# The gate modulation of the second layer is asked for when attention begins

## The chip, the core and the metric

The kernel runs on one core of one Trainium2 chip. The metric is the device time of one execution in microseconds (us). TensorE (PE in the profile) does matrix products and transposes, VectorE (DVE) and ScalarE (ACT) elementwise work and reductions, GpSimd (POOL) some elementwise work, and SyncE (SP) issues nearly all DMA transfers. Each engine works through its own list of instructions in order, and so does each list of transfers.

## The reference

Two layers run one after the other on `x` (1024 rows of 1024). Each is one mixer with three groups of heads between two norms:

```python
def hybrid_layer(x, c_act, ...):
    mod = c_act @ w_mod + b_mod
    shift, scale, gate = jnp.split(mod[:, None, :], 3, axis=-1)
    h = rms_norm(x, pre_gain) * (1.0 + scale) + shift
    proj = h @ w_in                     # 3088 columns, cut into the three groups' inputs
    a_out = sliding_window_attention(aq, ak, av, sinks) * silu(ag)
    r_out = rms_norm(retention(rq, rk, rv)) * silu(rg)
    g_out = rms_norm(gated_linear_attention(gq, gk, gv, log_a), gn) * silu(gg)
    y = concat([a_out, r_out, g_out]) @ w_out
    return x + gate * rms_norm(y, post_gain)
```

`c_act` is one row of 1024, the same for both layers. `w_mod` has 3072 columns per layer: a third each for shift, scale and gate. Shift and scale are needed when a layer starts; the gate, multiplied with `post_gain`, is needed only when the layer's rows are written.

## The kernel before

**Order of a layer.** The 1024 rows are eight tiles of 128, handled as four pairs. For a layer, `layer(l)` writes in this order: the projections `gg` and `rg` with their SiLU gates; then retention (projections `rq`, `rk`, `rv`, one chunk for each tile); gated linear attention, GLA (`gqk`, `gv`, with `kv` in between); attention (`aq0`, `aq1` with the rotation in `attn_rot`, then `ag0`, `ag1` with the gate); and the output product with `w_out`. In the second layer the last output (`last_output`) uses fewer products, over sums and differences of blocks of `w_out` and of pairs of rows, which VectorE, ScalarE and GpSimd prepare (`sw_second`, `Pair`).

**Precision.** The large products are three passes over operands that were split into a rounded high part and the rest. Each weight unit of 256 columns is loaded in four transfers of 256 KB into staging buffers `st` (eleven of them, shared by all weights, those of the modulation too), then split: ScalarE or VectorE writes the high part (line 147 or 149) and VectorE or GpSimd the rest (line 535).

**The planner.** TensorE's order is the order in which the program is written out; the other engines' lists are put in order by a scheduler that simulates when work can run. The writing is itself planned. `clk` is a clock in planned microseconds that each matmul advances by its estimated cost. Work beside the large products lives in generators, the jobs. A job yields a lag, and `pump`, called after every seven 256-column matmuls, every four 512-column ones, or after a product, lets each job go on whose lag has passed on `clk`. Flags order jobs among themselves. The lags are the dictionary `L`: a key with `@1` is used where the layer is 1 (the second one), the plain key otherwise.

**The modulation.** `mod_third(l, j)` computes one third (j = 2 is the gate) in two halves of 512 columns. Each half has eight steps: a transfer of 256 KB of `w_mod` into `st`, and a multiply-add on VectorE into the accumulator `acc` (line 365; line 363 for a first step without bias), then lag `mod2`. After lag `mod3` TensorE adds `acc` over the partitions. For the gate GpSimd first clears `acc` (line 357), SP loads the bias row into it (line 358), and the result is multiplied with the post gain into `modg` (line 379); then lag `mod5`. `acc` has one buffer, so a half begins only when TensorE has read the half before. `mod_all(l, js)` is a job that runs thirds one after another, if wanted after a flag. In each layer it is started after the gates, that is, when retention begins; in the first layer a second job waits for the first's flag and computes shift and scale of the second layer.

```python
            for k in range(KT):
                wt = stage()
                dma("lwm", wt, wv[:, k, c0:c0 + 512])
                ...
                    V.scalar_tensor_tensor(acc, wt, c_act[:, k:k + 1], acc, ALU.mult, ALU.add)
                yield lat("mod2", l)
            yield lat("mod3", l)
```

**Other names that the prediction uses.** `attn_rot` multiplies projected queries with tables read from memory (line 861), shifts 32-row blocks by transfers on SP (line 877), and a later job splits them (lines 835 and 836); TensorE's scores need that split. `attn_q` does the softmax of one tile; its probabilities go to TensorE through ScalarE (line 147) and an affine select on GpSimd (line 937). Attention output is stored in memory, read back and gated (line 1584; lags `aq5` and `ag1`). Head norms of retention and GLA wait lag `hn1` before TensorE transposes them. `kept` (line 1335) copies a product that later sums need.

Of the kernel before, what the change touches and what calls it, by code (L numbers as in the profile page):

```python
# [20 lines left out]
DEPTH = 2  # L21
# [70 lines left out]
def trunk(ctx: ExitStack, tc: tile.TileContext, ins, cst, out):  # L92
# [200 lines left out]
    def mod_first(rws, between):  # L293
# [20 lines left out]
        for hh in range(2):  # L314
# [9 lines left out]
            for k in range(KT):  # L324
# [271 lines left out]
    def sw_second():  # L596
        drain()
        for k in range(4):
# [7 lines left out]
            sw_split("T4", k, s4, "t4")  # L606
            yield L["sw1"]
        for name in ("T2", "T3", "T4"):
# [48 lines left out]
    def pre(l, t, xt, early=False, soon=False):  # L657
# [186 lines left out]
    def attn_kv(l, t, pk):  # L844
        kr = t1()[:, 0:P]
        v = kv["v"]
        v[t] = gp.tile([P, P], F32, tag="va", name=nm("va"), bufs=VDB)
        A.activation(v[t], pk[:, 128:256], AF.Copy)
# [33 lines left out]
    def attn_run(l):  # L882

        for hf in range(2):
            for g in range(2):
                for t in range(4 * hf, 4 * hf + 4):
                    yield (lat("aq7" if hf else "aq1", l), ("q", l, hf, g))
                    yield (0.0, ("kT", l, t))
                    job(attn_q(l, t, g, kv[(hf, g)]))
# [570 lines left out]
    def layer(l):  # L1460
# [25 lines left out]
                load(l, "rq")  # L1486
            gates_done[l] += n

        job(mod_all(l, (2,)))
        if l + 1 < DEPTH:  # L1490
            job(mod_all(l + 1, (1, 0), ("mod", l, 2)))
        for p in range(NP_):
            job(gla_decays(l, p))
        G.memset(stR, 0.0)
# [71 lines left out]
            do_kv(p)  # L1566
        load(l, "ag0")
        job(attn_run(l))
        mx = {}

        def rows(d, hf, *i):
# [96 lines left out]

B2, B1, BS, BST, MMB, SMB = 10, 8, 11, 5, 3, 3
EN = {"shw0": "V", "shw1": "A", "shw2": "A", "shw3": "A", "slw0": "V", "slw1": "G", "slw2": "V", "slw3": "G", "sht2": "A", "sht3": "A", "sht4": "A", "slt2": "V", "slt3": "G", "slt4": "G", "sd": "V", "mh0": "A", "mh1": "A", "mh2": "A", "mh3": "A", "mf": "A", "ms0": "V", "ms1": "V", "ms2": "V", "ms3": "V", "yg0": "V", "yg1": "V", "ml0": "V", "ml1": "V", "ml2": "V", "ml3": "V", "mod0": "A", "mod1": "V", "qst": "S", "smh": "S", "sml": "S", "sm0": "S", "sm1": "S", "lao": "S", "sao": "S", "lmix": "S", "ssg": "S", "lsg": "S", "ssr": "S", "lsr": "S", "lx": "S", "sx": "A", "lw": "S", "lwm": "S", "whi0": "V", "whi1": "A", "whi2": "A", "whi3": "A", "wlo0": "V", "wlo1": "V", "wlo2": "V", "wlo3": "G", "xn0": "V", "xn1": "V", "hlo0": "V", "hlo1": "V", "rot0": "V", "rot1": "V", "rdec": "V", "kslo": "V", "qslo": "V", "vlo": "G", "kT": "A", "qT": "A", "sprev": "A", "pn": "G", "pf0": "A", "aoc": "A", "hng": "V", "mh": "A", "gso": "V", "mg": "V", "mgl": "V", "rT": "A", "rv": "A", "gv": "A", "gk": "A", "ak0": "V", "ak1": "V", "ak2": "V", "ak3": "V", "kd0": "G", "kd1": "G", "kd2": "G", "kx1": "G", "kx2": "G", "kx3": "V", "kx4": "V", "qb": "G", "stx": "V"}  # L1670
L = {"sw1": 0.4, "ld1": 1.2, "ld2": 1.2, "ld1@1": 1.2, "ld2@1": 1.27, "swW00": 0.0, "swT1": 0.0, "swW11": 0.4, "swW10": 0.5, "tt1": 8.0, "tt2": 1.75, "tb1": 24.5, "tb2": 0.75, "pf3": 13.2, "pf1": 6.35, "pf2": 4.16, "mod1": 4.6, "mod2": 4.0, "mod3": 13.29, "mod4": 7.04, "mod5": 3.36, "mod6": 9.04, "pre1": 7.44, "kv1": 3.1, "kv2": 2.11, "aq1": 6.0, "aq7": 6.0, "ag1": 5.44, "aq2": 2.4, "aq6": 5.2, "aq3": 10.21, "aq4": 7.36, "aq5": 3.6, "hn1": 8.93, "hn2": 2.85, "gz1": 11.18, "gz2": 8.13, "gl1": 2.76, "gd3": 15.9, "gc1": 0.62, "gc2": 1.94, "gc3": 1.33, "gc4": 0.87, "gc6": 0.86, "gc5": 1.14, "rc1": 0.8, "rc2": 1.09, "rc3": 5.87, "rc4": 2.51, "fin1": 7.28, "lay1": 1.13, "gc4@1": 0.93, "mod2@1": 4.0, "mod3@1": 15.1, "mod5@1": 3.36, "mod6@1": 4.11, "pre1@1": 7.44, "kv1@1": 2.79, "kv2@1": 5.28, "aq1@1": 4.8, "aq7@1": 5.28, "ag1@1": 6.25, "aq2@1": 0.82, "aq6@1": 6.0, "aq3@1": 10.9, "aq4@1": 4.4, "aq5@1": 5.15, "hn1@1": 8.12, "hn2@1": 2.85, "gz1@1": 15.91, "gz2@1": 10.94, "gl1@1": 4.6, "gd3@1": 15.9, "gc1@1": 0.48, "gc2@1": 1.94, "gc3@1": 1.33, "gc6@1": 0.86, "gc5@1": 1.04, "rc1@1": 0.37, "rc2@1": 0.84, "rc3@1": 1.9, "rc4@1": 2.79, "fin1@1": 4.28, "lay1@1": 1.7}
CHUNK = 7
LAG = 2
VDB = 8
FIN = 1

_INS = ["x", "c", "positions", "w_mod", "b_mod", "pre_norm_gain", "post_norm_gain", "w_in", "attn_sinks",
# [29 lines left out]
```

## Time and profile before

| | |
|---|---|
| time, median of 3 runs | 1003.25 us (1001.63 to 1004.74) |
| profiled execution, time | 1010.63 us |
| profiled execution, span | 1008.9 us |
| mean granted TensorE clock | 0.986 |
| attention of the second layer, last product on TensorE ends | 920.8 us into the span |

A row of the profile names an engine, a source line, an operation and the tiles (output<-inputs, without buffer numbers). `x8` counts merged instructions; a bracket gives the idle time before the first of them and what ended it. Tables of waits give the total, the number and the longest. A line is often that of a helper: 163 is every matmul, 178 every transpose, 147 every copy on ScalarE, 152 every transfer through `dma`. The time of one row starts at the span's start. Busy time of TensorE is modelled, since matmuls are pipelined.

### The profile page before, as it was taken

What the parts mean: (1) busy time and instruction counts of PE and PEld (TensorE: products, weight loads), DVE (VectorE), ACT (ScalarE), POOL (GpSimd) and SP (SyncE); (2) the same over time, 40 slices, a digit from 0 to 9 for tenths busy, and PEclk for the clock granted to TensorE, in tenths of its full rate; (3) what the DMA queues carried; (4) which work ended last, traced back from release to release, by engine and by line L of the source; (5) the groups of instructions that cost most, each with busy time, mean ns of one, the idle gap of its engine ahead of it and who ended that gap; (6) DMA issues with size and microseconds to landing.
All of it is one profiled execution on the core that took longest, in us unless ns stands there. A gap on an engine that the chain in (4) does not pass through costs nothing.

```text
span 1008.9 us, 19610 instructions
## 1 busy us (share of the span) xinstructions
PE 975.4 (97%) x7137; PEld 829.5 (82%) x7137; DVE 684.5 (68%) x1680; ACT 408.8 (41%) x1152; POOL 234.4 (23%) x275
## 2 busy tenths in 40 slices
PE   5899999899999999999999999999999999999897
PEld 1499999888998777778889999998899877777785
DVE  3789857757666778564578275785666577566876
ACT  2476311223322656632465232123332256663321
POOL 2310001223320234330112000113332034544100
PEclk8899999999999999999999999999999999999999
DMA  9942513623326355577655251353132434378883
GB/s 293 308 137 76 173 45 100 170 81 96 96 74 199 89 149 163 171 239 244 214 157 173 64 158 32 108 150 100 41 104 85 125 90 130 112 236 249 265 263 140
DMA packets 129836, 148.73 MB, mean 147 GB/s; under 512 B 14046, under 2 KB 94152, under 8 KB 129740
## 3 DMA queue, kind: packets, MB, share of 16 engines
q1 hardware_dynamic: 124044, 137.92, 45.3%
q10 hardware_dynamic: 5696, 9.56, 2.6%
q8 instruction: 56, 0.92, 0.4%
q14 instruction: 40, 0.33, 0.1%
HBM read 109.17 MB, written 36.18 MB: 144 GB/s over the span
## 4 chain that ended last, share of the span: by engine, by line
PE 80%; DVE 8%; DMA 7%; issue 2%; POOL 1%; ACT 1%; SPq 0%; POOLq 0%; DVEq 0%; ACTq 0%
PE mm L163 61%; PE aux L163 14%; PE aux L178 5%; DMA st<-in_w_in_dram 2%; DMA st<-in_w_out_dram 1%; POOL sm L638 1%; DMA xk<-in_x_dram 1%; DMA wm<-in_w_mod_dram 1%; DMA t<-aoS 1%; DVE arena L535 1%; DMA st<-in_w_mod_dram 1%; DMA t<-sgS 1%; DVE t L328 0%; DVE st L572 0%; DMA mixF<-t 0%
## 5 line engine op out<-in xcount | busy, mean ns | idle before, releaser
L163 PE MATMUL mm<-arena 128*128 128x256 f32 (+2 forms) x1824 | 299.2, 318 | 1.8 <-ACT arena L707 1.8
L163 PE MATMUL mm<-arena,arena 128*128 128x256 f32 (+2 forms) x1824 | 300.7, 318 | 0.0
L163 PEld LDWEIGHTS mm<-arena 128*128 128x128 f32 x1824 | 254.6, 191 | 26.5 <-issue 4.1
L163 PEld LDWEIGHTS mm<-arena,arena 128*128 128x128 f32 x1824 | 254.1, 189 | 25.5 <-issue 4.6
L638 POOL TENSOR_TENSOR sm<-sm,mhalf 128x1 f32<-128x1 f32 (+1 forms) x64 | 56.1, 877 | 347.0 <-DVE sm L637 328.6
L163 PE MATMUL mm<-arena,mx 128*128 128x512 f32 (+1 forms) x564 | 132.4, 392 | 2.9 <-ACT kept L1335 2.9
L163 PEld LDWEIGHTS mm<-arena,mx 128*128 128x128 f32 x564 | 103.1, 191 | 27.1 <-ACT kept L1335 3.3
L147 ACT ACTIVATE t<-aux 128x256 f32<-128x256 f32 (+2 forms) x124 | 55.7, 467 | 76.1 <-PE aux L178 64.8
L147 ACT ACTIVATE arena<-st 128x512 fp32r<-128x512 f32 x94 | 56.1, 626 | 59.1 <-DMA st<-in_w_in_dram 21.4
L535 POOL TENSOR_TENSOR arena<-st,arena 128x512 fp32r<-128x512 f32 x31 | 43.2, 1395 | 138.9 <-ACT arena L147 100.9
L926 POOL TENSOR_TENSOR smx<-smx,sm 128x512 f32<-128x512 f32 x32 | 36.1, 1127 | 124.3 <-DVE sm L925 116.1
L535 DVE TENSOR_TENSOR arena<-st,arena 128x512 fp32r<-128x512 f32 x77 | 59.5, 795 | 6.1 <-ACT arena L147 4.1
L922 ACT ACTIVATE smx<-smx,sm 128x129 f32<-128x129 f32 x128 | 49.9, 392 | 28.4 <-DVE sm L919 28.4
L178 PE MATMUL aux<-c_ident,t 128*128 128x128 f32 (+1 forms) x292 | 48.8, 285 | 7.6 <-DVE t L669 7.2
L365 DVE SCALAR_TENSOR_TENSOR acc<-st,c_act,acc 128x512 f32<-128x512 f32 x60 | 45.5, 759 | 12.6 <-DMA st<-in_w_mod_dram 12.1
L178 PEld LDWEIGHTS aux<-c_ident,t 128*128 128x128 f32 (+1 forms) x292 | 35.4, 145 | 15.2 <-DVE t L669 9.0
L701 ACT ACTIVATE t<-aux,mod,mod 128x128 f32<-128x128 f32 x68 | 25.9, 458 | 43.8 <-DVE t L1242 18.2
L970 ACT ACTIVATE t<-aux 128x256 f32<-128x256 f32 x32 | 12.3, 383 | 75.5 <-PE aux L163 63.4
L163 PEld LDWEIGHTS aux<-t,mx 32*128 32x128 f32 (+1 forms) x896 | 39.5, 187 | 3.8 <-issue 2.1
L163 PE MATMUL aux<-t,mx 32*128 32x32 f32 (+1 forms) x896 | 40.7, 273 | 0.0
L917 DVE COPY_PREDICATED smx<-c_curmask,aux 128x256 f32<-128x256 int32 x64 | 25.5, 447 | 18.8 <-ACT smx L147 15.3
L1242 DVE SCALAR_TENSOR_TENSOR t<-t,sm,t 128x512 f32<-128x512 f32 x32 | 24.0, 779 | 18.6 <-DMA t<-in_x_dram 11.9
(220 smaller groups left out, 1384.3 us busy)
## 6 DMA issues: line engine op xcount, KB each, us to landing
st<-in_w_in_dram SPq DMA_DIRECT2D x96, 256.0 KB, 3.1
st<-in_w_mod_dram SPq DMA_DIRECT2D x64, 256.0 KB, 3.3
st<-in_w_out_dram SPq DMA_DIRECT2D x52, 256.0 KB, 3.8
mx<-mixS SPq DMA_DIRECT2D x20, 512.0 KB, 6.2
mixS<-t SPq DMA_DIRECT2D x72, 128.0 KB, 2.3
wm<-in_w_mod_dram SPq DMA_DIRECT2D x12, 512.0 KB, 8.0
t<-in_x_dram SPq DMA_DIRECT2D x24, 256.0 KB, 4.8
t<-tabS SPq DMA_DIRECT2D x16, 256.0 KB, 3.7
```

Of the source, the lines that this page charges most:

```text
L147: A.activation(dst, src, AF.Copy)
L163: T.matmul(dst, lhsT, rhs, start=start, stop=stop)
L178: T.transpose(dst, src, idn)
L365: V.scalar_tensor_tensor(acc, wt, c_act[:, k:k + 1], acc, ALU.mult, ALU.add)
L535: e.tensor_tensor(lo, st, f(hi), ALU.subtract)
L638: G.tensor_tensor(r, r, mhalf[:, :w], ALU.pow)
L701: A.activation(hf[:, ks], at[kt], AF.Identity, scale=gain, bias=shift)
L917: V.copy_predicated(sv, curmask.unsqueeze(1).to_broadcast((P, 2, P)), pv[:, :, n // P - 1, :])
L922: A.activation(sm[:, h, :], sm[:, h, :], AF.Exp, bias=mx[:, h:h + 1], accum_out=sums[:, h:h + 1])
L926: eng("pn").tensor_tensor(sm[:, :, 0:128], sm[:, :, 0:128], rs.unsqueeze(2).to_broadcast((P, 4, P)), ALU.mult)
L970: A.activation(sq, po, AF.Square)
L1242: V.scalar_tensor_tensor(xt[j], yg[j], r, xt[j], ALU.mult, ALU.add)
```

## The change

A tuple `EARLY` names the layers in which the modulation jobs start where they did, after the gates. In the other layers they start after attention's job. With `EARLY = (0,)` the first layer keeps its place for both jobs, and the second layer's gate third moves behind `attn_run`. Twenty lags get other values; all but `sw1` and `swW11` are those of the second layer. `mod2@1` is also used by the shift and scale of the second layer, which are computed during the first. No instruction is added or taken away.

```diff
@@ layer(l), after the gates
-        job(mod_all(l, (2,)))
-        if l + 1 < DEPTH:
-            job(mod_all(l + 1, (1, 0), ("mod", l, 2)))
+        if l in EARLY:
+            job(mod_all(l, (2,)))
+            if l + 1 < DEPTH:
+                job(mod_all(l + 1, (1, 0), ("mod", l, 2)))
@@ layer(l), before the attention projections
         load(l, "ag0")
         job(attn_run(l))
+        if l not in EARLY:
+            job(mod_all(l, (2,)))
+            if l + 1 < DEPTH:
+                job(mod_all(l + 1, (1, 0), ("mod", l, 2)))
@@ the lags L, those that differ
-sw1 0.4    swW11 0.4   ld1@1 1.2   ld2@1 1.27  gc4@1 0.93  mod2@1 4.0  mod6@1 4.11  kv1@1 2.79  kv2@1 5.28  ag1@1 6.25
+sw1 0.06   swW11 0.63  ld1@1 1.32  ld2@1 1.34  gc4@1 0.74  mod2@1 1.44 mod6@1 6.28  kv1@1 3.84  kv2@1 5.81  ag1@1 7.51
-aq2@1 0.82 aq5@1 5.15  hn1@1 8.12  gz2@1 10.94 gd3@1 15.9  gc2@1 1.94  gc3@1 1.33   gc6@1 0.86  rc4@1 2.79  fin1@1 4.28
+aq2@1 1.8  aq5@1 6.14  hn1@1 17.56 gz2@1 9.15  gd3@1 9.54  gc2@1 1.83  gc3@1 1.17   gc6@1 1.72  rc4@1 4.83  fin1@1 5.35
+EARLY = (0,)
```

More of the change, by code (lines that the diff above doesn't have):

```diff
@@ new lines @@
+L = {"sw1": 0.06, "ld1": 1.2, "ld2": 1.2, "ld1@1": 1.32, "ld2@1": 1.34, "swW00": 0.0, "swT1": 0.0, "swW11": 0.63, "swW10": 0.5, "tt1": 8.0, "tt2": 1.75, "tb1": 24.5, "tb2": 0.75, "pf3": 13.2, "pf1": 6.35, "pf2": 4.16, "mod1": 4.6, "mod2": 4.0, "mod3": 13.29, "mod4": 7.04, "mod5": 3.36, "mod6": 9.04, "pre1": 7.44, "kv1": 3.1, "kv2": 2.11, "aq1": 6.0, "aq7": 6.0, "ag1": 5.44, "aq2": 2.4, "aq6": 5.2, "aq3": 10.21, "aq4": 7.36, "aq5": 3.6, "hn1": 8.93, "hn2": 2.85, "gz1": 11.18, "gz2": 8.13, "gl1": 2.76, "gd3": 15.9, "gc1": 0.62, "gc2": 1.94, "gc3": 1.33, "gc4": 0.87, "gc6": 0.86, "gc5": 1.14, "rc1": 0.8, "rc2": 1.09, "rc3": 5.87, "rc4": 2.51, "fin1": 7.28, "lay1": 1.13, "gc4@1": 0.74, "mod2@1": 1.44, "mod3@1": 15.1, "mod5@1": 3.36, "mod6@1": 6.28, "pre1@1": 7.44, "kv1@1": 3.84, "kv2@1": 5.81, "aq1@1": 4.8, "aq7@1": 5.28, "ag1@1": 7.51, "aq2@1": 1.8, "aq6@1": 6.0, "aq3@1": 10.9, "aq4@1": 4.4, "aq5@1": 6.14, "hn1@1": 17.56, "hn2@1": 2.85, "gz1@1": 15.91, "gz2@1": 9.15, "gl1@1": 4.6, "gd3@1": 9.54, "gc1@1": 0.48, "gc2@1": 1.83, "gc3@1": 1.17, "gc6@1": 1.72, "gc5@1": 1.04, "rc1@1": 0.37, "rc2@1": 0.84, "rc3@1": 1.9, "rc4@1": 4.83, "fin1@1": 5.35, "lay1@1": 1.7}
```

1 line of the change is left out of this document (removed).

## The prediction

> **What bounds the kernel now.** I read the page first, then who waits for TensorE and when, then busy time by stretch, and last the instructions around each wait. The busy rows name the bound:
>
> ```profile
> span 1008.9 us, 19610 instructions
> PE 975.4 (97%) x7137; PEld 829.5 (82%) x7137; DVE 684.5 (68%) x1680; ACT 408.8 (41%) x1152; POOL 234.4 (23%) x275
> ```
>
> TensorE issues in the order that the planner wrote and is busy 97%, so a change that moves work between other engines can only give back, or create, moments in which TensorE waits. These are all of its named waits in the second layer (from 500 us), and then those of the first layer's second half (215 to 540 us):
>
> ```profile
> PE mm L163 <- ACT kept L1335: 2.9, 1, 2.9
> PE aux L163 <- ACT t L147: 1.3, 1, 1.3
> PE aux L163 <- DVE stR L1194: 1.0, 1, 1.0
> PE aux L163 <- DVE t L1173: 0.4, 1, 0.4
> ...
> PE aux L178 <- DVE mx L1115: 0.3, 1, 0.3
> PE aux L163 <- DVE sm L637: 0.3, 1, 0.3
> ```
>
> So the second layer loses TensorE time in two places: 2.7 us where retention ends and 2.9 us where the last output begins. By stretch (columns: us, then busy time and count for PE, PEld, DVE, ACT, POOL, then granted clock, DMA share, GB/s):
>
> ```profile
> 600.00:700.00 100.00, 97.32 (x778) 91.35 (x778) 64.40 (x186) 26.64 (x58) 17.26 (x18) 1.00 0.34 102
> 800.00:900.00 100.00, 100.00 (x608) 72.75 (x607) 69.06 (x136) 63.04 (x207) 41.81 (x44) 1.00 0.46 135
> 670.00:690.00 20.00, 17.32 (x118) 14.86 (x118) 11.78 (x28) 6.64 (x15) 4.59 (x4) 1.00 0.62 179
> 850.00:950.00 100.00, 97.11 (x524) 71.74 (x523) 68.45 (x127) 52.84 (x155) 41.22 (x42) 0.98 0.68 203
> 940.00:950.00 10.00, 7.11 (x24) 5.38 (x23) 9.35 (x19) 4.35 (x9) 0.49 (x2) 0.83 0.69 212
> ```
>
> The first two rows are the stage that the work leaves (retention) and the one that it enters (attention). Attention has no TensorE wait, but ACT and POOL are over twice as busy there. The wait at retention's end, on TensorE, ScalarE and the SP queue:
>
> ```profile
> 680.77 0.72 PE L163 MATMUL aux<-t 64*128 64x128 f32 x8 [1.28 <-ACT t L147]
> ...
> 679.60 0.63 ACT L147 ACTIVATE arena<-st 128x512 fp32r<-128x512 f32 x1 [3.77 <-DMA st<-in_w_in_dram]
> 680.14 0.58 ACT L147 ACTIVATE t<-aux 128x512 f32<-128x512 f32 x1
> ...
> 655.57 0.33 SPq L152 DMA_DIRECT2D t<-srS  x1
> 662.68 0.33 SPq L152 DMA_DIRECT2D st<-in_w_mod_dram  x1
> 664.80 0.38 SPq L152 DMA_DIRECT2D st<-in_w_in_dram  x1
> ...
> SPq L358 <- POOL acc L357: 9.3, 1, 9.3
> SPq L152 <- DVE stR L1194: 7.0, 1, 7.0
> ```
>
> Read upward. TensorE waits for ScalarE's copy at 680.14 (queries and keys of a retention chunk). That copy stands behind a weight conversion that sat 3.77 us for its transfer. The weights come through the SP queue, which is in order, and that queue stood still twice for the modulation: 9.3 us for the bias row into the accumulator (line 358), and 7.0 us before the modulation weights at 662.68, with the next w_in load (664.80) behind them.
>
> **The change part by part.** *The moved job.* Sixteen weight loads of 256 KB, two bias rows, two gain rows, two POOL memsets, sixteen sums on VectorE (line 365), four TensorE matmuls and two products (line 379) leave the stretch from about 577 to 703 us and enter the one from about 787 us. On SP the twenty transfers are 20 x 0.33 = 6.6 us of issue time (the row at 662.68 has one), which attention's shifts and stores now queue among. The count of work is the same, so only waits count. Removed: the two SP blocks and the sums between the retention chunks. I take the whole idle time of the 670 to 690 row, 20.00 - 17.32 = 2.68, as gone: **-2.7**. Bounds: 0 (the conversions alone keep it) and -2.7 (there is no more).
>
> *Late sums in attention.* One accumulator buffer serves all halves, so a half's sums can start only after the half before it was multiplied on TensorE, and TensorE stands still if they aren't ready at its own place. Before, the planner put 3.36 + 8 x 4.0 + 15.1 = 50.46 of its microseconds between two halves; now 3.36 + 8 x 1.44 + 15.1 = 29.98. What a planned microsecond is on the chip:
>
> ```profile
> 300.22 0.95 PE L163 MATMUL aux<-c_ones,acc 128*128 128x1 f32 x8
> 361.40 0.95 PE L163 MATMUL aux<-c_ones,acc 128*128 128x1 f32 x8
> 429.42 1.05 PE L163 MATMUL aux<-c_ones,acc 128*128 128x1 f32 x8
> 488.70 0.95 PE L163 MATMUL aux<-c_ones,acc 128*128 128x1 f32 x8
> 639.14 1.02 PE L163 MATMUL aux<-acc,c_ones 128*128 128x512 f32 x2
> 701.83 1.02 PE L163 MATMUL aux<-acc,c_ones 128*128 128x512 f32 x2
> ...
> 674.62 0.74 DVE L365 SCALAR_TENSOR_TENSOR acc<-st,c_act,acc 128x512 f32<-128x512 f32 x1
> 397.13 0.74 DVE L365 SCALAR_TENSOR_TENSOR acc<-st,c_act,acc 128x512 f32<-128x512 f32 x1
> 398.39 1.19 DVE L365 SCALAR_TENSOR_TENSOR acc<-st,c_act,acc 128x512 f32<-128x512 f32 x1
> ```
>
> Gaps of 61.18 (300.22 to 361.40), 59.28 and 62.69 us for 50.46 planned give 1.17 to 1.24, so the new gap is an estimated 35.2 to 37.3 us. The slowest sums took 675.36 - 639.14 = 36.2 us in the second layer and 399.58 - 361.40 = 38.2 us in the first layer's attention. So the wait is between 0 and 38.2 - 35.2 = +3.0; I take **0**, since the second layer's own 36.2 lies in the middle of the new gap. The first half's accumulator is free long before, so its sums can be done ahead. The same shorter lag holds for the second layer's shift and scale (mod2@1 serves them too, in the first layer's time): again 0 to +3.0, taken as 0, covered by 0.6 us of waits in all in that part and by the fact that they are now asked for when the queue is emptier than in the row at 398.39.
>
> *The first scores.* The new loads stand in the SP queue before the four shifts of the first rotated queries, and its margin is small:
>
> ```profile
> 801.77 1.28 DVE L836 TENSOR_TENSOR mx<-t,mx 128x512 fp32r<-128x512 f32 x2
> 803.26 0.74 PEld L163 LDWEIGHTS aux<-kT,mx 64*128 64x128 f32 x12 [0.36 <-issue]
> ```
>
> The split ends at 803.05, the scores start at 803.26: 0.2 us. Two sums ahead of it on VectorE would cost 2 x 0.74 = 1.5 us. But aq2@1 goes from 0.82 to 1.8, which puts these scores 0.98 planned us later (1.1 to 1.2 by the same ratio). Between 0 and +1.5; taken as 0, since the lag pays for most of it.
>
> *The last output.* TensorE's longest wait, with the row before it, and the VectorE row that the delay runs through:
>
> ```profile
> 939.77 3.68 PE L163 MATMUL mm<-arena,ma 128*128 128x512 f32 x15
> 946.33 3.92 PE L163 MATMUL mm<-arena,mx 128*128 128x512 f32 x9 [2.89 <-ACT kept L1335]
> ...
> 909.26 0.69 DVE L1584 SCALAR_TENSOR_TENSOR t<-t,t 128x512 f32<-128x512 f32 x1 [2.27 <-DMA t<-aoS]
> ```
>
> After the wait the clock is 0.83 in that 10 us row: nine matmuls took 3.92, where nine of the fifteen before took 9/15 x 3.68 = 2.21, so the stop costs 2.89 + 1.71 = 4.6 us. VectorE is 9.35 of 10 busy there. It had stood 2.27 us at 909.26 for a read of stored attention output, with the splits of w_out behind it. ag1@1 (6.25 to 7.51) and aq5@1 (5.15 to 6.14) put that read and that product 2.25 planned us later, so the splits can pass them. Bounds: 0 and -4.6. I take half of the 2.27, **-1.1**: nearer to nothing, because VectorE's waits for w_out transfers in the same stretch remain.
>
> *The other lags* (head norm hn1@1 8.12 to 17.56, decays gd3@1 15.9 to 9.54, the gc, gz, kv, rc, ld and fin1 entries, sw1) add no instruction: they change at which pump a job's next part is written. A pump comes every four or seven matmuls, so steps under about a planned microsecond often change nothing; swW11 and mod6@1 have no reader that is waited for in the second layer. Taken as 0: the list of waits above has none between 703 and 940 us, and the cover is that slack. If longer-held head norms run the tile buffers short, retention's and GLA's ScalarE copies would be late next.
>
> **The sum.** -2.7 + 0 + 0 + 0 - 1.1 = -3.8 us. On the profiled execution (1010.63 us, 7.4 above the median of 1003.25) that is 1006.8; on the median, 1003.25 - 3.8 = 999.45, **999.5 us**. 0.3%, some 3.0 us, is about what a measurement of this kernel tells from no change.
>
> **The rivals.** *The wait stays* (no change). The conversion at 679.60 waits for w_in, not for modulation weights, and 670 to 690 us is also where three weight units arrive at once (DMA share 0.62). For: the first layer waits in the same place, and there too for a ScalarE copy behind a conversion:
>
> ```profile
> 199.62 1.23 PE L163 MATMUL aux<-t 64*128 64x128 f32 x8 [3.09 <-ACT t L147]
> 198.19 0.63 ACT L147 ACTIVATE arena<-st 128x512 fp32r<-128x512 f32 x1 [2.87 <-DMA st<-in_w_in_dram]
> ```
>
> Against: modulation runs beside that retention too. Time: 1003.25 - 1.1 = 1002.2.
>
> *The last output pays* (slower). If the second half's loads stand behind the shifts and stores of attention until about 890 us, its eight sums (8 x 0.74 = 5.9 us) fall on VectorE where it is the bound (9.35 of 10 busy), and each is then TensorE time: 1003.25 - 2.7 + 5.9 = 1006.5 (rounded up from 1006.45). For: DMA share is 0.68 from 850 to 950 us. Against: by the gap above the half ends near 787 + 2 x 37 = 861 us. It decides from the point where more than 2.7 us of sums, four of them, come after 890; with a blocked SP queue w_out would be late as well.
>
> *Two engines on one port.* VectorE's sum at 398.39 took 1.19 us against 0.74 while POOL was in a subtraction of 1.74, and an affine select in attention is as tight as this:
>
> ```profile
> 397.30 1.74 POOL L535 TENSOR_TENSOR arena<-st,arena 128x512 fp32r<-128x512 f32 x1 [0.44 <-ACT arena L147]
> 887.25 1.30 POOL L937 TENSOR_SCALAR_AFFINE_SELECT t<-t 128x512 f32<-128x512 f32 x1 [3.92 <-ACT t L147]
> 888.83 0.60 PE L163 MATMUL aux<-t,vd 128*64 128x256 f32 x4
> ```
>
> It ended at 888.55, 0.28 us before its matmul. Sixteen sums at POOL's 0.42 share meet it 6.7 times, at 0.45 us each 3.0 us: if all reach TensorE, 999.45 + 3.0 = 1002.5; in retention POOL's share is 0.17. This is the rule of the Trainium skill (SBUF — State Buffer, section "SBUF: two separate sides"): VectorE with two SBUF inputs and GpSimd take one port pair in turn, each for a whole instruction. By that rule the move is to the wrong stage; the trace agrees in the 1.19 us row, but TensorE had no wait there.
>
> **How the numbers follow.** Forecast 0.46 (995.9 to 1001.5), the wait stays 0.13, port 0.08, the last output pays 0.33, this last at 1004 to 1008. Faster takes the forecast and a little of the other two: 0.48; same, what they leave with the forecast's edge: 0.17; slower 0.35 (the last rival, and both late-sum waits together). Low end: -2.7 - 4.6 is 995.95, less the 1.6 by which the fastest run shown lies under the median: 994.3. High end: 1006.5 and the first scores' +1.5: 1008.0.
>
> **What the new profile would show.** Right: no named wait of TensorE between 660 and 703 us, no SP wait on the memset of line 357 there, sums (line 365) from about 775 to 860, no wait before the accumulator's matmuls, and a wait under 2.9 us where the last output begins. Wrong: a wait on line 147 still at retention's end; TensorE waiting for a line 365; scores waiting for line 836; or a stop before the last output longer than 2.9 us, with sums or w_mod loads after 880 us.

## The result, and the profile after

The changed kernel is slower: 1015.75 us median (4 executions, 1013.88 to 1018.53) against 1002.89 us (1001.63 to 1004.74) for the kernel before on the same chip, a ratio of 1.0129 with a 95% interval of 1.0099 to 1.0159. The prediction was 999.5 (994.3 to 1008.0). The profiled execution took 1016.71 us.

The execution of the kernel before that the prediction read (1010.63 us) turned out to be untypical: a later one of the same code (e1 below) took 1002.69 us. From here on "before" in comparisons of traces is that later one. Its span, and the longest of its waits of TensorE between 660 and 705 us, and then from 790 us to the end:

```profile
span 1001.0 us, 19610 instructions
...
PE aux L163 <- ACT t L147: 1.5, 1, 1.5
PE aux L163 <- DVE stR L1194: 0.4, 1, 0.4
...
PE mm L163 <- DMA a<-mixS: 1.5, 2, 1.0
```

The wait at retention's end is in both executions. The 2.9 us for `kept` ahead of the last output, on which I had put 1.1 us of gain and the low end of the range, is not: it is 0.3 us here, and two waits for a transfer stand near it.

The changed kernel's page begins with these rows (busy us and share by engine):

```profile
span 1015.0 us, 19619 instructions
...
PE 980.8 (97%) x7137; PEld 833.8 (82%) x7137; DVE 679.1 (67%) x1680; ACT 407.4 (40%) x1152; POOL 230.8 (23%) x275
```

The work and the shares are those of before. The longest of TensorE's waits, from 690 us on and then from 215 to 540 us (engine, tile and line, what it waited for; total, number, longest):

```profile
PE mm L163 <- ACT kept L1335: 2.6, 1, 2.6
PE aux L163 <- POOL t L937: 1.6, 2, 0.9
PE aux L163 <- DVE t L963: 0.4, 1, 0.4
PE aux L163 <- ACT t L1099: 0.4, 1, 0.4
...
PE aux L178 <- DVE mx L1115: 1.1, 1, 1.1
PE aux L163 <- DVE mx L1115: 0.9, 1, 0.9
PE aux L163 <- DVE stG L1137: 0.6, 1, 0.6
```

The old wait for line 147 at retention's end is gone. In its place stand small waits in both layers' GLA, two in attention behind GpSimd's affine select, and one at the last output. By stretch (busy time and count for PE, PEld, DVE, ACT, POOL, then granted clock, DMA share, GB/s):

```profile
600.00:700.00 100.00, 100.00 (x806) 94.87 (x805) 58.73 (x180) 26.41 (x56) 16.95 (x17) 1.00 0.21 63
670.00:690.00 20.00, 20.00 (x143) 17.90 (x141) 12.42 (x34) 7.47 (x17) 3.96 (x4) 1.00 0.54 163
800.00:900.00 100.00, 98.21 (x585) 70.55 (x586) 69.22 (x143) 59.48 (x193) 38.06 (x41) 1.00 0.50 154
945.00:957.00 12.00, 9.36 (x29) 7.07 (x29) 10.68 (x22) 4.16 (x9) 0.60 (x2) 0.73 0.68 209
```

Where the time came from, stage by stage. The table gives how much later than before the same event is on the chip, worked out from the starts of the same rows in the two traces.

| event | before, us | changed: later by |
|---|---|---|
| first layer, last masked retention scores (line 1173) | 196.6 | 1.9 |
| first layer, last masked copy of GLA (line 1115) | 284.0 | 9.3 |
| second layer, first SiLU gate | 536.1 | 8.7 |
| second layer, last masked retention scores | 680.2 | 4.0 |
| second layer, last masked copy of GLA | 762.1 | 7.6 |
| second layer, last softmax maximum | 898.3 | 11.2 |
| end of the span | 1001.0 | 14.0 |

So the second layer's gates and retention did get 4.7 us shorter. About half of the loss arises where no moved instruction is, in the first layer's GLA (7.4 us), and the rest behind retention.

The waits alone are too short for 14 us. From 200 us on, TensorE's named waits above 0.35 us add to 8.0 us in the changed kernel and 3.8 before, a difference of 4.2. The larger part is the clock: behind such a wait TensorE often runs at a granted clock of 0.50, for 3.4 us or a multiple of it. While TensorE has work, this happens in the changed kernel at 226.9 (6.8 us), 704.7 (3.4) and 950.5 (6.8), before only at 196.7 (3.4). If half of such a time is lost, that is an estimated 8.5 us against 1.7. Waits and clock make 11.0 of the 14.0, and 1.9 lay ahead of them already; 1.1 us I cannot assign.

**The first layer's GLA** shows how such a wait comes about. In the changed kernel, VectorE, TensorE, and the stretch behind:

```profile
225.49 0.75 DVE L365 SCALAR_TENSOR_TENSOR acc<-st,c_act,acc 128x512 f32<-128x512 f32 x1 [0.67 <-DMA st<-in_w_mod_dram]
226.16 0.89 DVE L1115 COPY_PREDICATED mx<-c_mask,aux 128x128 f32<-128x128 int32 x4
...
226.51 2.95 PE L163 MATMUL aux<-t,mx 32*128 32x32 f32 x45 [0.87 <-DVE mx L1115]
...
227.00:233.50 6.50, 6.50 (x67) 6.44 (x68) 4.06 (x11) 0.68 (x4) 2.32 (x5) 0.50 0.22 65
```

and before:

```profile
222.68 0.90 DVE L1115 COPY_PREDICATED mx<-c_mask,aux 128x128 f32<-128x128 int32 x4 [1.06 <-ACT mx L1114]
224.35 0.75 DVE L365 SCALAR_TENSOR_TENSOR acc<-st,c_act,acc 128x512 f32<-128x512 f32 x1 [0.78 <-DMA st<-in_w_mod_dram]
...
227.00:233.50 6.50, 6.50 (x67) 6.17 (x65) 5.00 (x15) 0.81 (x3) 2.38 (x5) 1.00 0.29 91
```

Both times a sum of the modulation (line 365) waits some 0.7 us at the head of VectorE's list for its weights. Before, it stands behind the masked copy that TensorE needs, and nobody notices. After, it stands ahead of it: the copy is late, TensorE waits 0.87 us, and its small matmuls then run at 0.50. `mod2@1`, 1.44 instead of 4.0, writes the sums earlier, and the scheduler queued them earlier; e4 below tests that.

**Attention.** One of the two waits for the affine select (rows of VectorE, GpSimd, TensorE):

```profile
836.00 1.50 DVE L365 SCALAR_TENSOR_TENSOR acc<-st,c_act,acc 128x512 f32<-128x512 f32 x1
837.42 0.68 DVE L919 TENSOR_REDUCE sm<-smx 128x4 f32<-128x516 f32 x1
...
840.57 1.04 POOL L926 TENSOR_TENSOR smx<-smx,sm 128x512 f32<-128x512 f32 x1 [2.74 <-DVE sm L925]
841.56 0.64 POOL L937 TENSOR_SCALAR_AFFINE_SELECT t<-t 128x512 f32<-128x512 f32 x1
...
842.25 0.65 PE L163 MATMUL aux<-t,vd 128*64 128x256 f32 x4 [0.95 <-POOL t L937]
```

The sum takes 1.50 us and stands ahead of a softmax maximum. GpSimd waits 2.74 us for the reciprocal that follows from it, with the affine select of another tile queued behind, and TensorE waits for that. No run here takes this sum alone away.

**The last output.** TensorE and ScalarE:

```profile
951.15 5.49 PE L163 MATMUL mm<-arena,mx 128*128 128x512 f32 x12 [2.64 <-ACT kept L1335]
...
950.52 0.58 ACT L1335 ACTIVATE kept<-mm 128x512 f32<-128x512 f32 x1
```

The wait is nearly as long as the one that I read in the first trace of before, and the row 945 to 957 us above shows a mean clock of 0.73 there.

### The profile page after: what moved, and what is told of

Same layout as the page of the kernel before. It is cut to its first block, busy times and chain, and to the rows that moved or that the text cites. A ratio compares the mean times of both kernels' runs of the same rounds, so it can differ in the third digit from the quotient of the medians.

```text
span 1015.0 us, 19619 instructions
## 1 busy us (share of the span) xinstructions
PE 980.8 (97%) x7137; PEld 833.8 (82%) x7137; DVE 679.1 (67%) x1680; ACT 407.4 (40%) x1152; POOL 230.8 (23%) x275
## 4 chain that ended last, share of the span: by engine, by line
PE 76%; DVE 9%; DMA 8%; issue 3%; POOL 2%; ACT 2%; SPq 0%; POOLq 0%; DVEq 0%; ACTq 0%
PE mm L163 58%; PE aux L163 14%; PE aux L178 4%; DMA st<-in_w_in_dram 2%; DMA st<-in_w_mod_dram 2%; DMA st<-in_w_out_dram 1%; POOL sm L638 1%; DMA t<-aoS 1%; DVE acc L365 1%; DMA mixS<-t 1%; DMA t<-tabS 1%; ACT arena L147 0%; POOL arena L535 0%; DVE t L328 0%; DMA posi<-in_positions_dram 0%
## 5 line engine op out<-in xcount | busy, mean ns | idle before, releaser
L163 PE MATMUL mm<-arena 128*128 128x256 f32 (+2 forms) x1824 | 302.7, 320 | 1.8 <-ACT arena L707 1.8
L926 POOL TENSOR_TENSOR smx<-smx,sm 128x512 f32<-128x512 f32 x32 | 35.7, 1115 | 134.2 <-DVE sm L925 122.2
L365 DVE SCALAR_TENSOR_TENSOR acc<-st,c_act,acc 128x512 f32<-128x512 f32 x60 | 49.1, 818 | 11.8 <-DMA st<-in_w_mod_dram 11.3
L535 DVE TENSOR_TENSOR arena<-st,arena 128x512 fp32r<-128x512 f32 x77 | 55.1, 738 | 2.0 <-PE mm L163 1.1
L163 PEld LDWEIGHTS aux<-t,mx 32*128 32x128 f32 (+1 forms) x896 | 42.3, 194 | 6.8 <-issue 2.3
L163 PE MATMUL aux<-t,mx 32*128 32x32 f32 (+1 forms) x896 | 43.8, 279 | 2.1 <-DVE mx L1115 0.9
```

What stands on the lines that cost most here:

```text
L163: T.matmul(dst, lhsT, rhs, start=start, stop=stop)
L535: e.tensor_tensor(lo, st, f(hi), ALU.subtract)
L926: eng("pn").tensor_tensor(sm[:, :, 0:128], sm[:, :, 0:128], rs.unsqueeze(2).to_broadcast((P, 4, P)), ALU.mult)
```

## The experiments

All ratios are against the kernel before on the same chip in the same sequence of runs.

| run | median, us | ratio, 95% interval |
|---|---|---|
| e1 before again | 1004.52 | 1.0011 (0.9999 to 1.0024) |
| e2 move only | 1018.22 | 1.0137 (1.0115 to 1.0159) |
| e3 lags only | 1023.62 | 1.0202 (1.0165 to 1.0239) |
| e4 modulation steps as before | 1010.40 | 1.0082 (1.0054 to 1.0110) |
| e5 and GLA's lags | 1013.24 | 1.0088 (1.0059 to 1.0116) |
| e6 and attention's lags | 1013.90 | 1.0116 (1.0065 to 1.0166) |
| e7 move, narrow sums | 1017.01 | 1.0126 (1.0088 to 1.0163) |
| e8 gate at the layer's start | 1014.15 | 1.0096 (1.0069 to 1.0124) |
| e9 gate not counted | 1007.64 | 1.0042 (1.0017 to 1.0067) |
| e10 move, TensorE's order kept | 1012.60 | 1.0085 (1.0058 to 1.0111) |
| e11 rc4 alone | 1004.44 | 1.0006 (0.9984 to 1.0028) |
| e12 e10 with fast steps | 1015.29 | 1.0111 (1.0084 to 1.0139) |
| e13 e10 with sums held back | 1005.85 | 1.0031 (1.0016 to 1.0047) |
| e14 hn1 alone | 1009.41 | 1.0060 (1.0039 to 1.0080) |
| e15 hn1 and rc4 | 1004.28 | 1.0008 (0.9984 to 1.0033) |
| e16 e13 with hn1 and rc4 | 1003.91 | 1.0010 (0.9991 to 1.0029) |
| e17 e4 with sums held back | 1016.56 | 1.0107 (1.0063 to 1.0150) |
| e18 e17 with the old phase | 1018.19 | 1.0135 (1.0103 to 1.0168) |

**The two parts of the change, each alone.** e1 has no edit.

> The kernel before, unchanged, to get a second trace of it. Its only profile so far is of an execution 7.7 us above its own median (1010.63 against 1002.89), so a stage table against the changed kernel may be off. If the profile of before was simply a slow one at some place that the changed kernel does not have, a second trace of about 1003 us shows the difference of some 13 us stage by stage; if executions with a profile are always slower, the new one is near 1010 us again. Ratio 1.000 either way.

e2 makes the move and keeps the old lags:

```diff
+        if l in EARLY: ...        # EARLY = (0,), as in the change; L as before
```

> Only the move (EARLY = (0,)), all lags as before, so mod2 stays at 4.0. Theory LAGS (the loss comes from the new lags; the move alone gives back the wait where retention ends): 998 to 1001 us. Theory MOVE (the sums and loads beside attention cost more than they free in retention): 1006 to 1016 us, with waits of TensorE between 790 and 870 us.

e3 has the new lags and no move:

```diff
-L = {... "mod2@1": 4.0, ... "hn1@1": 8.12, ...}
+L = {... "mod2@1": 1.44, ... "hn1@1": 17.56, ...}     # all twenty as in the change
```

> Only the new lags, the gate modulation stays where it was, after the gates (though with mod2 at 1.44 its two halves come closer). Theory LAGS: 1012 to 1018 us, with the same extra waits in both linear attentions as the changed kernel has. Theory MOVE: 1000 to 1006 us.

Each part alone loses: 1.0137 and 1.0202. The two losses don't add. e3, in which the last sum of the gate starts at 629 us, shows in its waits from 790 us on that the last output suffers under the new lags with no moved sum about:

```profile
PE mm L163 <- DVE kept L1339: 4.2, 1, 4.2
PE aux L163 <- POOL t L937: 2.0, 2, 1.3
```

In e2 retention's wait is still there (2.5 us for line 147), so the move did not remove it. Its longest new wait is this one in the second layer's GLA:

```profile
765.02 0.33 PE L178 MATMUL aux<-c_ident,t 128*128 128x128 f32 x1 [2.48 <-DVE mx L1115]
```

**Which of the lags.** e4 is the changed kernel with the modulation's own two lags as before, e5 that with GLA's too, e6 that with those of attention and `w_out`:

```diff
 e4: -"mod2@1": 1.44, "mod6@1": 6.28      +"mod2@1": 4.0, "mod6@1": 4.11
 e5: also gd3@1, gc2@1, gc3@1, gc4@1, gc6@1 as before
 e6: e4 with kv1@1, kv2@1, aq2@1, aq5@1, ag1@1, ld1@1, ld2@1, sw1 as before
```

> The changed kernel with mod2@1 back at 4.0 and mod6@1 at 4.11: shift and scale of the second layer are summed at the old pace during the first layer, and so is the moved gate. Theory MOD2 (denser sums and loads in the first layer's linear attention hold up VectorE there; +5 us between 226 and 300 us in the traces): 1008 to 1011 us. Theory of the other lags or of the move: 1014 to 1017 us.

> The changed kernel with mod2@1 and mod6@1 as before and also the five lags of the second layer's linear attention (gd3, gc2, gc3, gc4, gc6). Theory GLA-LAGS (they start TensorE's linear-attention blocks before VectorE has their inputs: waits of 0.7 us at about 692 and 750 us in the run with mod2 as before): both waits go, 1007 to 1009.5 us against 1010.4. Theory that those waits come from the other changes around them: they stay, 1010 to 1012 us.

> The changed kernel with mod2@1 and mod6@1 as before and the lags of attention and of the loads as before (kv1, kv2, aq2, aq5, ag1, ld1, ld2, sw1). In the run with mod2 as before attention and the last output lost some 12 us against the kernel before (785 to 945 us). Theory ATTENTION-LAGS: that goes, 1000 to 1003 us. Theory SUMS (the moved sums and loads hold up VectorE, GpSimd and with them the value products): it stays, 1008 to 1012 us, with waits at the value products between 830 and 900 us.

e4's ratio is 0.47% below the changed kernel's (1.0082 against 1.0129), some 4.7 us, though the two intervals just overlap. The trace is clearer: its first layer's GLA has one wait of 0.2 us left from 215 to 540 us, no half clock, and ends 1.9 us ahead of before (which has its half-clock spell at 196.7) instead of 9.3 behind, and e3, with `mod2@1` at 1.44 and no move, has a wait of 1.55 us and 6.8 us of half clock at the same place as the changed kernel. That part of the loss is `mod2@1`: `mod6@1`, which e4 also puts back, only delays a flag behind a finished third, and the first product of these sums is at 275 us. Behind the first layer's GLA, e4 loses 7.8 us in its trace and the changed kernel 4.7, so its second layer is no better. Neither e5 nor e6 brings more. Each moves waits: with GLA's lags as before, 0.4 us at 692 goes, and 0.4 us at 751 becomes 0.8 and 0.4 us at 772 comes; with attention's, 1.7 us at 835 go and 1.8 us at 768 come, and 2.7 us at 877 to 879 become 3.8 us in four waits from 868 to 887.

**Sums or place.** e7 is e2 with the moved sums of one column (it leaves out the sums of the other 511 columns of the second layer's gate, so its result is not the layer's). e8 is the kernel before with the second layer's gate job at the head of the layer:

```diff
 e7: -acc, wt, c_act[:, k:k + 1], acc             +acc[:, 0:1], wt[:, 0:1], c_act[:, k:k + 1], acc[:, 0:1]
 e8: +if l == 1: job(mod_all(l, (2,)))            # first in layer(1), and not after the gates
```

> Only the move, all lags as before, and the gate's sixteen sums of the second layer (the first step of a half included) touch one column instead of 512: what is left out is the rest of these sums, so the gate is wrong beyond a few columns; every load, wait and order stays. The move alone lost 11 us in the second layer's linear attention (700 to 770 us) and 3 us later. Theory SUMS (VectorE time of 0.75 us each in the way): 1002 to 1006 us. Theory LOADS/ORDER (the queue and the order of the lists cost, not the sums' duration): 1012 to 1018 us.

> The kernel before, all lags as before, with the second layer's gate job started at the head of the layer instead of after its gates, so that both halves are done before the end of retention. Theory RETENTION (the waits of 3.2 us where retention ends come from the second half's loads and sums there): they go, 999 to 1001.5 us. Theory that any other order than the tuned one loses: 1005 to 1015 us.

e7 is as slow as e2, and TensorE has nearly the same wait for the masked copy there (2.4 us against 2.5). On VectorE:

```profile
766.36 0.22 DVE L366 SCALAR_TENSOR_TENSOR acc<-st,c_act,acc 128x1 f32<-128x1 f32 x1 [2.90 <-DMA st<-in_w_mod_dram]
766.50 0.89 DVE L1116 COPY_PREDICATED mx<-c_mask,aux 128x128 f32<-128x128 int32 x4
```

(Lines are one higher in this kernel.) A sum of 0.22 us does the same harm as one of 0.75: the 2.90 us that it waits for its weights are the cost, with the copies behind it. e8 loses too, though its sums are over at 602 us: it has 1.4 us at 540, 3.1 us at retention's end and 1.7 us in three waits from 727 to 760 us.

**The planner's phase.** The gate's products advance the planner's clock; without them the small blocks behind fall at other pumps. e9 leaves everything where it was and takes one product's planned 0.85 us off that clock. e10 is e2 with a job that does nothing but advance the clock by the gate's products at their old place, while the real ones are not counted: in the traces, TensorE's 7137 matmuls stand in the order of before but for the gate's own four. e12 is e10 with the moved job stepping every 1.44.

```diff
 e9:  -mult(pm, allones, acc, True, True)   +mult(pm, allones, acc, True, True, 0.0 if l == 1 and hh == 1 else None)
 e10: e2, and
      -mult(pm, allones, acc, True, True)   +mult(pm, allones, acc, True, True, 0.0 if l == 1 else None)
      +if l == 1: job(ghost())              # old lags; clk[0] += 4 * 512 / 2400.0 for each half
 e12: e10, and  -yield lat("mod2", l)       +yield 1.44 if l == 1 and j == 2 else lat("mod2", l)
```

> The kernel before, with all lags and places as before; only the planner's clock does not count the 0.853 planned us of the second layer's last gate product. The work is the same, and TensorE's order differs only in where the linear attention of the second layer's small blocks stand among the large products. Theory PHASE (the small blocks were placed to the pump, and any shift of the planner's clock puts two of them back to back before their inputs are there; short waits in these thin matmuls then also halve the granted clock): 1008 to 1014 us, with waits near 719, 742 and 762 us as in the move alone. Theory SUMS/LOADS: 1002 to 1005 us.

> Only the move, all lags as before, with the planner's clock kept in step: a job without work counts the gate's products at the old place, and the moved ones are not counted. TensorE's order is that of before except for the two gate products. Theory PHASE: the loss in the linear attention (700 to 770 us; 11 us in the move alone) goes; what is left is the move itself, 1003 to 1007 us, and the wait where retention ends stays, as it did in the move alone. Theory SUMS/LOADS: 1010 to 1017 us.

> As the move with the order kept, but the moved gate job alone steps at 1.44, as in the changed kernel, while shift and scale step at 4.0. Its two products stand among the first half of attention, at the places that the prediction worked out. Theory LATE SUMS (TensorE waits for the second half's sums): 1 to 3 us above the move with the order kept, with a wait at the gate's product. Theory that the sums are ready: within 1.5 us of it.

e9 costs 0.4% with no instruction moved but those blocks. Its waits from 705 to 790 us, where the same list of before is empty:

```profile
PE aux L178 <- DVE mx L1115: 0.7, 1, 0.7
PE aux L163 <- ACT t L1099: 0.5, 1, 0.5
```

e10's ratio is 0.52% below e2's, and the intervals don't meet: phase is a part of the move's price. It still loses 0.85%, with this on VectorE and TensorE, and behind it the clock:

```profile
760.34 0.75 DVE L365 SCALAR_TENSOR_TENSOR acc<-st,c_act,acc 128x512 f32<-128x512 f32 x1 [2.01 <-DMA st<-in_w_mod_dram]
761.01 0.89 DVE L1115 COPY_PREDICATED mx<-c_mask,aux 128x128 f32<-128x128 int32 x4
...
761.36 0.33 PE L178 MATMUL aux<-c_ident,t 128*128 128x128 f32 x1 [2.21 <-DVE mx L1115]
...
763.10:769.70 6.60, 6.60 (x61) 6.54 (x62) 3.46 (x12) 1.55 (x7) 0.46 (x1) 0.50 0.57 178
```

It is the picture of the first layer and of e7 again: a sum waits for its weights at the head of VectorE's list, with the masked copies of the last GLA block behind it. In the program's text the moved job starts after attention's, but its lags run out and the scheduler queues it while GLA's last block is still open. In e12 the waits at 759 to 763 us are 2.7 us, and 2.0 us more come at 839 to 841 us, where its sums now meet the softmax. It is 2.7 us slower than e10, but the intervals overlap.

**The sums held back.** e13 is e10 with the job waiting for the last masked copy, and its sums ordered behind that copy on VectorE:

```diff
-                V.copy_predicated(scz[:, c, h, :], mask2, ...)
+                held[l, p] = V.copy_predicated(scz[:, c, h, :], mask2, ...)
+        flag(("scz", l, p))
+                    with tc.issue_after(held[l, NP_ - 1].ins):       # second layer's gate
+                        V.scalar_tensor_tensor(acc, wt, c_act[:, k:k + 1], acc, ALU.mult, ALU.add)
-            job(mod_all(l, (2,)))
+            job(mod_all(l, (2,), ("scz", l, NP_ - 1)))
```

> The kernel of the move with TensorE's order kept, and one thing more: the moved gate's job starts when the last first-pass scores of the second layer's gated linear attention have been written, and its sums are queued on VectorE behind the copy that writes them (line 1115 in the kernel before). TensorE's order is the one of the kernel with the order kept. Theory 'a sum at the head of VectorE's queue': there, VectorE waited 2.0 us at 758 us for a weight chunk of the modulation (sum at 760.34), the masked copies behind it came late, TensorE waited 2.2 us for them and then ran at a clock of 0.50 for 6.8 us (3.4 us lost). So here no TensorE wait for the masked copy at 755 to 765 us, no half-clock spell at 763, and a time of 1012.6 - 5.6 = about 1007. Rival 'the sums cost wherever they lie' (port, transfers, tiles held): the wait goes but returns in attention, 1011 to 1015. Rival 'the wait is another's': VectorE's sums are behind the copies and TensorE still waits over 1.5 us there, 1012 to 1013.

1005.85 us, and the interval lies below e10's. The last masked copy, the first sums, and the stretch that ran at 0.50 in e10:

```profile
763.04 0.90 DVE L1120 COPY_PREDICATED mx<-c_mask,aux 128x128 f32<-128x128 int32 x4 [2.09 <-ACT mx L1119]
...
765.09 1.53 DVE L368 SCALAR_TENSOR_TENSOR acc<-st,c_act,acc 128x512 f32<-128x512 f32 x2
...
763.10:769.70 6.60, 6.60 (x62) 6.39 (x61) 5.44 (x22) 2.00 (x9) 0.97 (x2) 1.00 0.49 144
```

(Lines are five or three higher in this kernel: 1120 is 1115, 368 is 365.) VectorE now waits for ScalarE, TensorE does not wait, and the clock stays at 1.00. TensorE's matmuls stand in the same order in e10 and e13, so that is not the difference. At the last softmax maximum e13 is 0.2 us behind before, where e10 is 6.2 us. So the 1.37% that the move costs alone is 0.52% phase (e2 to e10), 0.54% sums ahead of GLA's copies (e10 to e13), and 0.31% that is left. e13 starts the moved loads later too, and no run separates that from the place of the sums.

**Retention's end.** Where the changed kernel and e3 to e6 have no wait for line 147, they all have the new `hn1@1` and `rc4@1`. e11 is the kernel before with one of them, e14 with the other, e15 with both, and e16 is e13 with both:

```diff
 e11, e15, e16: -"rc4@1": 2.79   +"rc4@1": 4.83
 e14, e15, e16: -"hn1@1": 8.12   +"hn1@1": 17.56
```

> The kernel before with one lag changed, rc4@1 from 2.79 to 4.83 (the flag of the retention state comes two planned us later). Theory LAG (the changed kernel's gain at retention's end comes from this lag and not from the move): the waits of 2 to 3 us between 670 and 700 us go, 999 to 1002 us. Theory MOVE: they stay, 1003 to 1006 us.

> The kernel before with one lag of the second layer changed, the head norm's transpose behind its output (hn1@1 8.12 to 17.56 planned us); the gate stays beside retention. In every kernel with the new lags the waits at retention's end (674 to 697 us, about 3.2 us in the kernel before) are gone, in every kernel with the move alone they stay, and the lag rc4@1 alone leaves 2.2 us of them. Theory 'hn1@1 frees retention's end': no TensorE wait above 0.4 us between 665 and 700 us, and 1000 to 1002 if nothing else moves. Rival 'phase': the small blocks of the second layer's gated linear attention fall at another place and new waits of 1 to 4 us with half-clock spells come behind 700 us, 1004 to 1012, whatever retention gains. Rival 'both lags are needed': 2 us or more of waits left at 665 to 700 us.

> The kernel before with both lags of the second layer's retention as in the changed kernel (hn1@1 17.56, rc4@1 4.83), the rest and the gate as before. Theory 'the two lags free retention's end': no TensorE wait above 0.4 us between 665 and 700 us; 1000 to 1002 if the rest holds, more where the blocks behind them come to other places. Rival 'the gate's sums keep the wait': over 1.5 us of waits remain there as long as the sums are beside retention, 1004 or more.

> The move with the sums held behind the last masked copy (as in the run of that name) and the two retention lags of the changed kernel (hn1@1 17.56, rc4@1 4.83). If both parts do what their theories say, no wait at retention's end (3 us less than with the sums held alone) and none for the masked copy at 755 to 765 us: 1003 to 1005. If retention's freed time comes back as waits in the second layer's gated linear attention or in attention, 1007 to 1012.

The wait at retention's end in e14, and what is left of it in e15:

```profile
676.63 0.77 PE L163 MATMUL aux<-t 64*128 64x128 f32 x8 [3.07 <-ACT t L147]
```

```profile
674.31 0.78 PE L163 MATMUL aux<-t 64*128 64x128 f32 x8 [0.37 <-ACT t L147]
```

`hn1@1` alone does not shorten it (before had 1.3 and 1.5 us, e9 2.5), and `rc4@1` alone leaves 0.9 us at 676. Both together leave next to nothing, with the gate's sums still beside retention in e15: it takes both. Yet no gain shows: e15 and e16 are within 0.1% of before. Of the 2.3 us of waits at retention's end e15 has 0.4 left, but 0.8 us come at 756 and 0.4 at the last output, and the rest is less than these runs can tell. The two also show what a wait costs. TensorE's wait and the stretch behind it in e15, then in e16:

```profile
756.02 1.38 PE L163 MATMUL aux<-t,mx 32*128 32x32 f32 x41 [0.81 <-DVE t L963]
...
757.60:767.60 10.00, 10.00 (x128) 9.35 (x127) 4.77 (x24) 2.62 (x13) 0.47 (x1) 1.00 0.21 57
```

```profile
755.01 1.38 PE L163 MATMUL aux<-t,mx 32*128 32x32 f32 x41 [0.81 <-DVE t L968]
...
757.60:767.60 10.00, 10.00 (x89) 9.71 (x88) 3.57 (x13) 1.24 (x6) 0.46 (x1) 0.50 0.19 58
```

The same 0.81 us wait among the same matmuls is followed by full clock in one execution and by 10.2 us of half clock in the other: an estimated 5.1 us apart, and the spans differ by 4.6 (1001.7 and 1006.3). e5 and e14 have a wait of 0.81 us for the same line, both without half clock behind it. e16 has the gate moved, and these runs cannot tell it from before.

**What is left in the changed kernel.** e17 is e4 with the moved job's start and its sums held back as in e13, e18 is e17 with the old phase as in e10.

> The changed kernel with the modulation steps as before (mod2@1 4.0, mod6@1 4.11: 1010.4 us as a run of its own) and the moved sums queued on VectorE behind the last masked copy of the second layer's gated linear attention. Theory 'what is left are the other new lags': in 1010.4 us the waits lie at 833 to 836 (1.9 us and 3.4 us of half clock), 875 to 877 (3.2 us) and 940 (3.8 us and 3.4 us of half clock), all behind the place where the hold acts, so it stays at 1008 to 1011. Rival 'the sums made those waits too', through transfers and VectorE's order in attention: 1003 to 1006.

> The same, and the planner's clock advances by the gate's products where they stood before the move, so that what is planned behind them keeps the old phase under the new lags. Theory 'phase': 1 to 4 us less than without it, as with the move alone (1018.2 to 1012.6). Rival 'the new lags set their own phase': the same within 2 us, or more.

Neither is faster than e4, and e17 lies above both ranges that were expected. In e17 these waits remain in attention and at the last output, and e18 has one of 6.06 us:

```profile
848.03 0.65 PE L163 MATMUL aux<-t,va 128*64 128x256 f32 x4 [1.69 <-ACT t L147]
...
888.25 0.65 PE L163 MATMUL aux<-t,va 128*64 128x256 f32 x4 [1.69 <-ACT t L147]
...
956.03 4.15 PE L163 MATMUL mm<-arena,mx 128*128 128x512 f32 x10 [3.16 <-ACT kept L1341]
```

```profile
962.04 5.37 PE L163 MATMUL mm<-arena,a 128*128 128x512 f32 x12 [6.06 <-DMA a<-mixS]
```

With the sums behind the copies and with the old phase, attention and the last output lose as much as ever. That leaves the other new lags as the likely source, and e3 agrees for the last output (4.2 us without the move); in attention it has only the waits for the affine select, so there the lags together with the moved job remain possible. Which of these lags it is stays open; e6, with eight of them as before, still lost 1.2%, and under the new lags the two edits that had helped the move alone brought nothing. No version here beats the kernel before.

## Why the prediction was wrong, point by point

The sum was -3.8 us; the measured change is +12.9. The step that failed is "the count of work is the same, so only waits count" as it was carried out: I priced the waits that I saw in the old order, took every new place in a list as free, and left out the half clock behind a wait. By the table above, gates and retention gained 4.7 us, and the first layer's GLA (7.4), the second layer's GLA (3.6), attention (3.6) and the last output (2.8) lost 17.4.

*Retention, -2.7 for the modulation's hold on the SP queue.* The size was right by luck (0 busy time lost from 670 to 690 us), the cause wrong. With no modulation load and no sum beside retention, e13 still has, on ScalarE and TensorE:

```profile
675.93 0.63 ACT L147 ACTIVATE arena<-st 128x512 fp32r<-128x512 f32 x1 [2.70 <-DMA st<-in_w_in_dram]
...
677.10 0.72 PE L163 MATMUL aux<-t 64*128 64x128 f32 x8 [1.92 <-ACT t L147]
```

The conversion waits for its own weights, as the rival "the wait stays" had it. What frees TensorE is two lags which I had priced at nothing (e15). They write retention's chunks elsewhere among the products. In the changed kernel ScalarE's copy then stands ahead of that conversion; in e15, with these two lags alone, it still stands behind one, which waits only 1.07 us. These are ScalarE's rows in the changed kernel:

```profile
674.43 0.60 ACT L147 ACTIVATE t<-aux 128x512 f32<-128x512 f32 x1 [0.89 <-PE aux L178]
675.43 0.63 ACT L147 ACTIVATE arena<-st 128x512 fp32r<-128x512 f32 x1 [0.40 <-DMA st<-in_w_in_dram]
```

*Shift and scale with `mod2@1`, 0 (0 to +3.0).* This step failed most clearly. I looked for sums that come too late for their own product. They came too early, and delayed others' work on VectorE: 7.4 us in the first layer's GLA by the table, some 4.7 by e4's ratio. The four waits above 0.35 us there add to 3.0 us, just my bound; the half clock behind them, an estimated 3.4 us more, was not in it.

*Late sums in attention, 0 (0 to +3.0).* No product waited for a sum: the four matmuls of the accumulator stand without a wait. But the sums ran from 763.0 to 839.6 us, earlier than my 775 to 860, and at both ends of that stretch they stood ahead of what TensorE needed: GLA in e2, e7, e10 and e12, the softmax in the changed kernel. The forecast had asked what the sums wait for, and not what waits behind them.

*The first scores, 0 (0 to +1.5).* Right: no matmul of the changed kernel waits for line 836.

*The last output, -1.1 (0 to -4.6).* Wrong in sign. The `kept` wait of 2.64 us is there with a half clock of 6.8 us behind it. The trace that the step came from was an execution 7 us above the median, and the wait that I meant to shorten belongs to that execution: in the other one it is 0.3 us. It is not what made the 7 us: of the 7.9 us between the two spans, 5.3 had arisen by the last masked copy of the first layer's GLA (289.3 against 284.0), and only 1.8 came behind the last softmax maximum. I had noted the excess and not asked which rows made it. The rival "the last output pays" names the right place, but its mechanism is not what happened: no sum starts after 840 us, and e3 has the loss without the moved job.

*The other lags, 0.* Wrong as a class. "The waits list has none there" was taken as slack, while it only says that the present order has none. e9 shifts the planner's clock by 0.85 planned us and loses 0.4%; e14 changes one lag and loses 0.6%.

*Two engines on one port, +3.0.* The effect is in the rows: sums beside GpSimd's work take up to 1.53 us (at 825.47, beside a row of 1.40 on GpSimd) against a median of 0.75, as the Trainium skill has it (SBUF — State Buffer, section "SBUF: two separate sides": the two engines take one port pair in turn), and the one at 836.00 above is in a chain that ends in a TensorE wait. But e7, with sums of one column, is as slow as e2, so under the old lags it is not what the move costs; under the new ones that was not tried.

## What to carry to other kernels

A moved job is to be priced by what stands behind it in each in-order list, at both ends of its new place: an instruction that waits for a transfer makes everything behind it wait too, however short its own work. Where TensorE's order has no waits, that is not slack, and lags that add no instruction are changes of order with a price of their own. Before a wait is counted as a gain, see that it is in more than one execution, above all when the profiled one is above the median.

## What the runs showed of the hardware

A TensorE wait of under 1 us can cost several times its length. Behind 0.87 us at 226 us the clock was 0.50 for 6.8 us; behind 0.81 us in e16 for 10.2 us, and in e15 behind the same wait not at all. In the runs here these spells are 3.4, 6.8 or 10.2 us long, apart from the one that ends each execution, and all those between 200 and 800 us but one (e6 at 769) follow waits of 0.3 to 3.1 us around retention's and GLA's small matmuls. In each of the twenty traces all changes of the clock lie on one grid of 3.413 us, to within 0.003 us, and the grid lies differently against the program from one execution to the next (the first point of it behind TensorE's first matmul comes after 0.1 to 3.2 us). That fits the same wait costing much in one execution and nothing in another; which place on the grid is the bad one these traces do not settle. The Trainium skill (TensorE: Matmul & The Clock Gate, Part 1) states two rates, a half and a whole, and a window of about 3.4 us that runs freely; the 0.50 and the multiples of 3.4 agree with it. The practical rule of that page of the Trainium skill (section "Why this matters for your kernels"), to avoid idle gaps of more than about 3 us, does not cover these cases: no wait ahead of a spell in GLA was longer than 2.5 us here, and more than half of them were under 1.
